# Batched matmul with a transposed right side: six of GpSimd's fourteen stores moved behind the loads on the SP queue

## The chip, the cores and the metric

The kernel runs on one core of a Trainium2 chip; the program uses no other core. The metric is the device time of one execution in microseconds. The profile's span is about 1.8 us shorter than that time (124.1 against 125.88 us in the profiled execution of the kernel before). Every time quoted here comes from an execution whose trace was recorded.

## The reference

```python
batch, m, k, n = 16, 512, 512, 512          # a: [16, 512, 512], b: [16, 512, 512], f32
def reference(a, b):
    return np.matmul(a, b.transpose(0, 2, 1)).astype(np.float32)
```

The inputs are 33.55 MB and the output 16.78 MB, so 50.33 MB must move whatever is done.

## The kernel before

It works in eight pairs of batches. SP's queue loads 2 MB of `a` or `b` for a pair into one of seven slots `ld`. VectorE casts to bf16, TensorE transposes, VectorE and ScalarE copy the transposes to SBUF, TensorE multiplies, and ScalarE copies the sums from PSUM to one of seven output slots `ob`, 1 MB for each batch. The stores are the part that the change touches. GpSimd runs through the string `STORES`. An S waits until a batch is complete and issues its store. An O waits until the next store in turn has landed and hands its slot back to ScalarE.

```python
    STORES = "SSSSOSOSOSSOSOSOSOSOSOS"        # 14 S, 9 O
    LAST = 2                                  # the last two stores go on SP's queue
    ...
        # SP: loads; "s_go" hands a landed load to VectorE
        for n in range(NL):
            load(n)
        for n in range(2 * pairs):
            got = nc.sync.wait_ge(s_ld[n % NL], 16 * (n // NL + 1))
            ...                               # got.then_inc(s_go, ...)
            if n > 0 and n + NL - 1 < 2 * pairs:
                load(n + NL - 1)
        for n in range(batch - LAST, batch):
            nc.sync.wait_ge(s_out, n + 1)
            nc.sync.dma_start(
                out[n].rearrange("(p j) n -> p j n", j=J), ob[:, n % NO]
            ).then_inc(s_last[n % LAST], 16)
    ...
        # GpSimd: nothing before load 7 has landed, then the string
        nc.gpsimd.wait_ge(s_ld[0], 32)
        for what in STORES:
            if what == "S":
                slot = n_st % NO
                nc.gpsimd.wait_ge(s_out, n_st + 1)
                nc.gpsimd.dma_start(
                    out[n_st].rearrange("(p j) n -> p j n", j=J), ob[:, slot]
                ).then_inc(s_st[slot], 16)
                n_st += 1
            else:
                nc.gpsimd.wait_ge(s_st[n_of % NO], 16 * (n_of // NO + 1)).then_inc(s_of, 1)
                n_of += 1
    ...
    # after the closing barrier: the wait for the last store
        nc.sync.wait_ge(s_last[(batch - 1) % LAST], 16)
```

Of the kernel before, what the change touches and what calls it, by code (L numbers as in the profile page):

```python
# [10 lines left out]
def kernel(  # L11
# [6 lines left out]
    nc = tc.nc  # L18
    P = 128
    batch, M, K = a.shape  # L20
    _, N, _ = b.shape
    J = M // P
# [7 lines left out]
    NO = 7  # L30


    STORES = "SSSSOSOSOSSOSOSOSOSOSOS"
    LAST = 2

    def sbuf(name, shape, dtype):
        return ctx.enter_context(nc.sbuf_tensor(name, shape, dtype))

    def sem(name):
        return tc.alloc_semaphore(name)  # L40

    with tc.tile_critical(no_gpsimd_drain=True):  # L42
# [8 lines left out]
        ob = sbuf("ob", [P, NO, J, N], f32)  # L51
# [3 lines left out]
        s_set = sem("s_set")  # L55
        s_ld = [sem(f"s_ld{i}") for i in range(NL)]
        s_second = [sem(f"s_second{i}") for i in range(2)]
        s_last = [sem(f"s_last{i}") for i in range(LAST)]
        s_st = [sem(f"s_st{i}") for i in range(NO)]

        s_go = sem("s_go")
        s_of = sem("s_of")
# [12 lines left out]
        s_out = sem("s_out")  # L75
# [5 lines left out]
            out=ident[:], in_=ident[:], compare_op=mybir.AluOpType.not_equal, fill=1.0,  # L81
# [7 lines left out]
        def load(n):  # L89
            u, slot = n // 2, n % NL  # L90
            src = (a if n % 2 == 0 else b)[2 * u:2 * u + 2].rearrange(
                "e (p j) k -> (e p) j k", j=2 * J
            )
            if n >= NL:

                nc.sync.wait_ge(s_cd, n - NL + 2)
            if n < 2:
                nc.sync.dma_start(
                    ld[:, slot, :J, :], src[:, :J, :]
                ).then_inc(s_ld[slot], 16)  # L100
                nc.sync.dma_start(
                    ld[:, slot, J:, :], src[:, J:, :]
                ).then_inc(s_second[slot], 16)
            else:
                nc.sync.dma_start(ld[:, slot], src).then_inc(s_ld[slot], 16)

        for n in range(NL):
            load(n)
        for n in range(2 * pairs):
# [6 lines left out]

            if n > 0 and n + NL - 1 < 2 * pairs:
                load(n + NL - 1)

        for n in range(batch - LAST, batch):  # L120
            nc.sync.wait_ge(s_out, n + 1)
            nc.sync.dma_start(
                out[n].rearrange("(p j) n -> p j n", j=J), ob[:, n % NO]
            ).then_inc(s_last[n % LAST], 16)
        for n in range(batch - NO, batch - LAST):
            nc.sync.wait_ge(s_st[n % NO], 16 * (n // NO + 1))
        for n in range(batch - LAST, batch - 1):
            nc.sync.wait_ge(s_last[n % LAST], 16)


        n_st = n_of = 0
        nc.gpsimd.wait_ge(s_ld[0], 32)
        for what in STORES:
            if what == "S":
                slot = n_st % NO
                nc.gpsimd.wait_ge(s_out, n_st + 1)
                nc.gpsimd.dma_start(  # L137
                    out[n_st].rearrange("(p j) n -> p j n", j=J), ob[:, slot]
                ).then_inc(s_st[slot], 16)
                n_st += 1  # L140
            else:
                nc.gpsimd.wait_ge(s_st[n_of % NO], 16 * (n_of // NO + 1)).then_inc(s_of, 1)
                n_of += 1

        def taker(engine):
# [10 lines left out]
        with nc.Fori(0, pairs, engines=[dve]) as u:  # L156
            for x, (h, w, s_c, s_w) in enumerate(
# [4 lines left out]
                if x == 0:  # L162
# [3 lines left out]
                    out=h[:, :J, :], in_=src[:, :J, :HK]  # L166
# [4 lines left out]
                    out=h[:, J:, :], in_=src[:, J:, :HK]  # L171
                ).then_inc(s_c, 1)
                nc.vector.tensor_copy(  # L173
                    out=w[:, J:, :], in_=src[:, J:, HK:]
                ).then_inc(s_w, 1)
            for ko in range(KO):
# [5 lines left out]
                if ko == 1:  # L182
# [3 lines left out]
                    out=tb[:, ko, :],  # L186
# [9 lines left out]
        with nc.Fori(0, pairs, engines=[act]) as u:  # L196
            for ko in range(KO):
# [5 lines left out]
                for e in range(2):  # L203
                    c = nc.scalar.copy(  # L204
                        out=ta[:, ko, e * J * P:(e + 1) * J * P].rearrange(
                            "k (j p h) -> k j p h", j=J, h=2
                        ),
# [5 lines left out]
            for e in range(2):  # L213
                take(s_of, 1)
                dst = ob[:, bass.ds((u * 2 + e) % NO, 1)].rearrange("m o j n -> m (o j) n")
                for j in range(J):
                    if j < J - 1:
                        nc.scalar.wait_ge(s_mm, j + 1)
                    else:
# [3 lines left out]
                        out=dst[:, j, :].rearrange("m (p j) -> m p j", j=2 * J),  # L223
# [51 lines left out]


    with tc.tile_critical(no_gpsimd_drain=True):
        nc.sync.wait_ge(s_last[(batch - 1) % LAST], 16)


# [28 lines left out]
```

## Time and profile before

| | before |
|---|---|
| time, median of 3 | 125.86 us (125.82 to 125.87) |
| span of the profile | 124.1 us |
| data moved, mean rate | 50.33 MB, 406 GB/s |
| last data packet ends, fifteen DMA engines | 120.3 to 120.6 us |
| last data packet ends, the sixteenth | 122.24 us |

The page and the stretches by stage are shown with the prediction, below. Two more views are needed: the DMA issues with the median time from issue to landing, and the waits of SP's queue from 66 us on (who waited, for whom, us in total, times, longest).

```profile
out_dram<-ob POOLq DMA_DIRECT2D x14, 1024.0 KB, 24.1
out_dram<-ob SPq DMA_DIRECT2D x2, 1024.0 KB, 8.3
```

```profile
SPq L110 <- DMA ld<-in_b_dram: 22.2, 3, 7.4
SPq L122 <- ACT ob L222: 13.6, 2, 11.8
SPq L304 <- DMA out_dram<-ob: 1.7, 1, 1.7
```

The reader sees that GpSimd's stores take 24 us each from issue to landing (up to four are issued at once, and they share the engines with the loads), and that the last thing SP waits for, 1.7 us long, is the landing of the last store.

One reading of the trace is used all through this text and needs a name. In these traces a DMA reports its landing by 16 increments of a semaphore (544 for the 34 DMAs of the kernel before), and I read them as one from each DMA engine: of the last store of the kernel before, fifteen come from 120.6 to 121.0 us and one at 122.71, as fifteen engines end by 120.6 and one at 122.24. **The lag** is the time from the last but one of these to the last, read to about 0.01 us. **The excess** of a packet is what it took over the usual time of its size, 309 ns for 8 KB and 611 ns for 16 KB (the medians of the kernel before). The packet records do not number the engines, so the excess is summed over all of them; from 102 us on, the packets with an excess follow one another almost without overlap (from 102 to 114 us of the kernel before, 20 packets have an excess over 10 ns, and no two overlap by more than 13 ns), as those of a single engine do.

### The profile page before, as it was taken

What the parts mean: (1) busy time and instruction counts of PE and PEld (TensorE: products, weight loads), DVE (VectorE), ACT (ScalarE), POOL (GpSimd) and SP (SyncE); (2) the same over time, 40 slices, a digit from 0 to 9 for tenths busy, and PEclk for the clock granted to TensorE, in tenths of its full rate; (3) what the DMA queues carried; (4) which work ended last, traced back from release to release, by engine and by line L of the source; (5) the groups of instructions that cost most, each with busy time, mean ns of one, the idle gap of its engine ahead of it and who ended that gap; (6) DMA issues with size and microseconds to landing.
All of it is one profiled execution on the core that took longest, in us unless ns stands there. A gap on an engine that the chain in (4) does not pass through costs nothing. (4 is left out here: it accounts for less than half of the span.)

```text
span 124.1 us, 2416 instructions
## 1 busy us (share of the span) xinstructions
PE 92.3 (74%) x768; PEld 57.8 (47%) x768; DVE 70.2 (57%) x112; ACT 68.1 (55%) x130; POOL 9.5 (8%) x20
## 2 busy tenths in 40 slices
PE   0006299998999999899989998994699937995000
PEld 0005296467446744764574476343684426541000
DVE  0065677948992896589389478903878059400000
ACT  4005133589568845966695589336665196556000
POOL 2000000000000170002010220101010012100000
PEclk9999999999999999999999999999679999999965
DMA  4999999999999999999999999999999999999980
GB/s 79 401 428 431 452 423 438 423 428 423 433 433 423 428 433 396 433 407 449 417 428 449 409 441 425 420 441 420 449 415 417 428 431 428 425 425 423 428 338 11
DMA packets 4896, 50.33 MB, mean 406 GB/s; under 512 B 544, under 2 KB 544, under 8 KB 544
## 3 DMA queue, kind: packets, MB, share of 16 engines
q1 hardware_dynamic: 2880, 35.65, 68.2%
q0 software_dynamic: 2016, 14.68, 28.1%
HBM read 33.55 MB, written 16.78 MB: 406 GB/s over the span
## 5 line engine op out<-in xcount | busy, mean ns | idle before, releaser
L264 PE MATMUL ps<-tb,ta 128*128 128x512 bf16 x256 | 57.7, 379 | 0.4
L222 ACT COPY ob<-ps 128x512 f32 x64 | 34.4, 589 | 29.4 <-PE ps L264 26.2
L204 ACT COPY ta<-tp 128x512 bf16<-128x512 bf16 x64 | 32.9, 608 | 15.7 <-PE tp L245 15.7
L264 PEld LDWEIGHTS ps<-tb,ta 128*128 128x128 bf16 x256 | 24.1, 98 | 30.5 <-issue 3.9
L245 PE MATMUL tp<-ident,ha 128*128 128x128 bf16 x256 | 20.2, 236 | 12.5 <-PEq L146 12.5
L245 PE MATMUL tp<-ident,hb 128*128 128x128 bf16 x256 | 19.3, 235 | 8.3 <-PEq L146 8.2
L245 PEld LDWEIGHTS tp<-ident,ha 128*128 128x128 bf16 x256 | 17.5, 107 | 15.7 <-issue 14.0
L185 DVE COPY tb<-tp 128x1024 bf16<-128x1024 bf16 x32 | 21.3, 685 | 5.0 <-DVEq L146 4.8
L245 PEld LDWEIGHTS tp<-ident,hb 128*128 128x128 bf16 x256 | 17.1, 107 | 9.0 <-issue 9.0
L137 POOL DMA_DIRECT2D out_dram<-ob x14 | 8.8, 631 | 95.7 <-DMA out_dram<-ob 54.3
L165 DVE CAST hb<-ld 128x1024 bf16 x8 | 5.5, 688 | 12.8 <-DVEq L146 12.8
L180 DVE COPY ha<-wa 128x2048 bf16<-128x2048 bf16 x8 | 5.6, 694 | 10.1 <-DVEq L146 9.8
L165 DVE CAST ha<-ld 128x1024 bf16 x8 | 5.5, 690 | 6.6 <-DVEq L146 6.4
L170 DVE CAST hb<-ld 128x1024 bf16 x8 | 5.5, 685 | 1.1 <-DVEq L146 1.1
L170 DVE CAST ha<-ld 128x1024 bf16 x8 | 5.5, 688 | 1.0 <-DVEq L146 1.0
L184 DVE COPY hb<-wb 128x2048 bf16<-128x2048 bf16 x8 | 5.5, 685 | 0.5 <-DVEq L146 0.5
L168 DVE CAST wa<-ld 128x1024 bf16 x8 | 5.5, 687 | 0.0
L168 DVE CAST wb<-ld 128x1024 bf16 x8 | 5.5, 685 | 0.0
L173 DVE CAST wa<-ld 128x1024 bf16 x8 | 5.5, 683 | 0.0
L173 DVE CAST wb<-ld 128x1024 bf16 x8 | 5.5, 682 | 0.0
L195 ACT ACT_TABLE_LOAD x1 | 1.3, 1283 | 1.1 <-SPq L42 1.1
L80 POOL TENSOR_SCALAR_AFFINE_SELECT ident<-ident 128x128 bf16<-128x128 bf16 x1 | 0.3, 284 | 0.2 <-POOL ident L78 0.2
(6 smaller groups left out, 0.8 us busy)
## 6 DMA issues: line engine op xcount, KB each, us to landing
ld<-in_a_dram SPq DMA_DIRECT2D x7, 2048.0 KB, 30.1
ld<-in_b_dram SPq DMA_DIRECT2D x7, 2048.0 KB, 31.2
out_dram<-ob POOLq DMA_DIRECT2D x14, 1024.0 KB, 24.1
ld<-in_a_dram SPq DMA_DIRECT2D x2, 1024.0 KB, 6.0
ld<-in_b_dram SPq DMA_DIRECT2D x2, 1024.0 KB, 10.1
out_dram<-ob SPq DMA_DIRECT2D x2, 1024.0 KB, 8.3
```

The source lines that it names most:

```text
L137: nc.gpsimd.dma_start(out[n_st].rearrange("(p j) n -> p j n", j=J), ob[:, slot]).then_inc(s_st[slot], 16)
L165: nc.vector.tensor_copy(out=h[:, :J, :], in_=src[:, :J, :HK]).then_inc(s_cd, 1)
L168: nc.vector.tensor_copy(out=w[:, :J, :], in_=src[:, :J, HK:])
L170: nc.vector.tensor_copy(out=h[:, J:, :], in_=src[:, J:, :HK]).then_inc(s_c, 1)
L173: nc.vector.tensor_copy(out=w[:, J:, :], in_=src[:, J:, HK:]).then_inc(s_w, 1)
L180: nc.vector.tensor_copy(out=ha[:], in_=wa[:]).then_inc(s_ca, 1)
L184: nc.vector.tensor_copy(out=hb[:], in_=wb[:]).then_inc(s_cb, 1)
L185: nc.vector.tensor_copy(out=tb[:, ko, :], in_=tp[:, 2 + ko % 2].rearrange("k j p -> k (j p)"),).then_inc(s_eb, 1)
L204: c = nc.scalar.copy(out=ta[:, ko, e * J * P:(e + 1) * J * P].rearrange("k (j p h) -> k j p h", j=J, h=2), in_=tp[:, ko % 2, :, e * HP:(e ...
L222: c = nc.scalar.copy(out=dst[:, j, :].rearrange("m (p j) -> m p j", j=2 * J), in_=ps[:, j, :].rearrange("m (j p) -> m p j", j=2 * J),)
L245: t = nc.tensor.transpose(tp[:, 2 * x + g, j, :], h[:, j, g * P:(g + 1) * P], ident[:])
L264: t = nc.tensor.matmul(ps[:, j, :], ta[:, ko, (e * J + j) * P:(e * J + j + 1) * P], tb[:, ko, :].rearrange("k (j p) -> k j p", j=2 * J)[:, ...
```

## The change

Its intent is to use GpSimd's queue (`software_dynamic` on the page; SP's is `hardware_dynamic`) for the first eight stores only, and to let SP issue the other eight behind the loads. Stores 8 to 13 are placed in SP's loop after the hand-over of loads 11, 13 and 15. Each store gets a semaphore of its own.

```diff
-    STORES = "SSSSOSOSOSSOSOSOSOSOSOS"
-    LAST = 2
+    STORES = "SSSSOSOSOSSOOOOOO"
+    LATE = {11: (8, 9), 13: (10, 11), 15: (12, 13)}
...
+        def store(n):
+            engine = nc.gpsimd if n < STORES.count("S") else nc.sync
+            engine.wait_ge(s_out, n + 1)
+            engine.dma_start(
+                out[n].rearrange("(p j) n -> p j n", j=J), ob[:, n % NO]
+            ).then_inc(s_st[n], 16)
...
             if n > 0 and n + NL - 1 < 2 * pairs:
                 load(n + NL - 1)
-        for n in range(batch - LAST, batch):
-            ...
+            for m in LATE.get(n, ()):
+                store(m)
+        store(batch - 2)
+        store(batch - 1)
...
-                nc.gpsimd.wait_ge(s_st[n_of % NO], 16 * (n_of // NO + 1)).then_inc(s_of, 1)
+                nc.gpsimd.wait_ge(*landed(n_of)).then_inc(s_of, 1)
```

More of the change, by code (lines that the diff above doesn't have):

```diff
@@ L57 @@
         s_second = [sem(f"s_second{i}") for i in range(2)]
-        s_last = [sem(f"s_last{i}") for i in range(LAST)]
-        s_st = [sem(f"s_st{i}") for i in range(NO)]
+        s_st = [sem(f"s_st{i}") for i in range(batch)]
         s_go = sem("s_go")
@@ L105, in load, with landed @@
                 nc.sync.dma_start(ld[:, slot], src).then_inc(s_ld[slot], 16)
+        def landed(n):
+            return s_st[n], 16
+        def store(n):
[4 more added lines that the diff above has]
+            ).then_inc(s_st[n], 16)
         for n in range(NL):
@@ L118 @@
                 load(n + NL - 1)
-        for n in range(batch - LAST, batch):
-            nc.sync.wait_ge(s_out, n + 1)
-            nc.sync.dma_start(
-                out[n].rearrange("(p j) n -> p j n", j=J), ob[:, n % NO]
-            ).then_inc(s_last[n % LAST], 16)
-        for n in range(batch - NO, batch - LAST):
-            nc.sync.wait_ge(s_st[n % NO], 16 * (n // NO + 1))
-        for n in range(batch - LAST, batch - 1):
-            nc.sync.wait_ge(s_last[n % LAST], 16)
+            for m in LATE.get(n, ()):
+                store(m)
+        store(batch - 2)
+        store(batch - 1)
+        for n in range(batch - NO, batch - 1):
+            nc.sync.wait_ge(*landed(n))
         n_st = n_of = 0
@@ L134 @@
             if what == "S":
-                slot = n_st % NO
-                nc.gpsimd.wait_ge(s_out, n_st + 1)
-                nc.gpsimd.dma_start(
-                    out[n_st].rearrange("(p j) n -> p j n", j=J), ob[:, slot]
-                ).then_inc(s_st[slot], 16)
+                store(n_st)
                 n_st += 1
             else:
-                nc.gpsimd.wait_ge(s_st[n_of % NO], 16 * (n_of // NO + 1)).then_inc(s_of, 1)
+                nc.gpsimd.wait_ge(*landed(n_of)).then_inc(s_of, 1)
                 n_of += 1
@@ L277 @@
     with tc.tile_critical(no_gpsimd_drain=True):
-        nc.sync.wait_ge(s_last[(batch - 1) % LAST], 16)
+        nc.sync.wait_ge(*landed(batch - 1))
 _INS = ['a', 'b']
```

## The prediction

> **What bounds the kernel now.** I read the page first, then the stretches by stage, then the waits of the SP queue, then the order of time, and last the trace's records of DMA packets and of the 16 increments by which each DMA reports its landing. The page's first two parts and its DMA rows:
>
> ```profile
> span 124.1 us, 2416 instructions
> ...
> PE 92.3 (74%) x768; PEld 57.8 (47%) x768; DVE 70.2 (57%) x112; ACT 68.1 (55%) x130; POOL 9.5 (8%) x20
> ...
> DMA  4999999999999999999999999999999999999980
> ...
> q1 hardware_dynamic: 2880, 35.65, 68.2%
> q0 software_dynamic: 2016, 14.68, 28.1%
> HBM read 33.55 MB, written 16.78 MB: 406 GB/s over the span
> ```
>
> The reader is to see that no compute engine is near full, while the DMA row is at 9 (90% or more) from the second slice to the last but one. The two queues together hold 68.2 + 28.1 = 96.3% of the time of 16 DMA engines. The kernel is bound by its 50.33 MB, and the change moves not one byte less. The stretches (columns: stretch, its length, busy time and count by engine, granted clock, DMA share, GB/s):
>
> ```profile
> 4.00:43.00 39.00, 29.15 (x259) 20.21 (x260) 25.92 (x41) 20.69 (x40) 0.00 (x0) 1.00 1.01 431
> 47.00:99.00 52.00, 47.68 (x397) 29.30 (x395) 34.01 (x55) 33.39 (x65) 4.35 (x7) 0.97 1.00 427
> 103.00:112.00 9.00, 8.50 (x73) 4.93 (x71) 3.83 (x7) 5.28 (x12) 1.41 (x2) 1.00 1.01 425
> 116.00:118.00 2.00, 0.00 (x0) 0.00 (x0) 0.00 (x0) 0.00 (x0) 0.00 (x0) 1.00 1.03 434
> 118.00:120.20 2.20, 0.00 (x0) 0.00 (x0) 0.00 (x0) 0.00 (x0) 0.00 (x0) 0.62 1.02 432
> 120.70:122.20 1.50, 0.00 (x0) 0.00 (x0) 0.00 (x0) 0.00 (x0) 0.00 (x0) 0.50 0.05 22
> 122.30:124.10 1.80, 0.00 (x0) 0.00 (x0) 0.00 (x0) 0.00 (x0) 0.00 (x0) 0.50 0.00 0
> ```
>
> Loads alone (4 to 43), loads and GpSimd's stores together (47 to 99), GpSimd's stores alone (103 to 112) and the last SP stores (116 to 120.2) all run at 425 to 434 GB/s. So which queue carries a transfer does not set the rate. The sixth row is the one that matters: from 120.7 to 122.2 the DMA share is 0.05, about one sixteenth. **One DMA engine of sixteen works on after the other fifteen are done.** In the packet records the fifteen end between 120.3 and 120.6 us, and one ends at 122.24, finishing packets of 309 ns one by one.
>
> **Where that laggard comes from.** Each DMA reports its landing by 16 increments, one for each engine. For each landing I took the distance of the last increment from the last but one. For loads up to 42.8 us, when no store had yet been issued, it is 0.06 us or less. Then it grows: 0.30 us for the load that lands at 62.9, 0.68 at 77.9, 0.98 at 92.8, 1.09 at 100.2; for GpSimd's stores 1.11 at 102.5, 1.47 at 107.7, 1.69 at 115.3. The two last stores, which SP issues, have 1.69 (120.2) and 1.74 (122.7). So the lag begins when GpSimd's stores begin and is 1.7 us by the end: 1.7 / 14 stores = 0.12 us per store on GpSimd's queue, and between the two SP stores it grows by 0.05 only. The packets themselves do not last longer on GpSimd's queue: its 8 KB packets take 309 ns at the median, and so do the 8 KB packets on SP's.
>
> [...] 427 GB/s with both queues against 431 with one. [...] loads go in 16 KB packets (612 ns), stores in 8 KB packets (309 ns), so a store should get a third of the rate, 1.05 MB / (428 / 3 GB/s) = 7.35 us; GpSimd's stores land at 55.3, 62.6, 69.9, 77.2, 84.6, 91.9, 99.2 us, every 7.3 us. [...] an engine falls behind with GpSimd's stores, but one only, and the records do not number it.
>
> **The change, part by part.**
> 1. Removed from GpSimd's queue: stores 8 to 13, six of fourteen DMAs (631 ns of issue each, 3.8 us on an engine that is 8% busy: worth nothing). Added to SP's queue: the same six, at about 0.35 us of issue each (the two that SP issues now take 343 and 347 ns). No byte, matmul or copy changes; the order of instructions on PE, DVE and ACT is the same.
> 2. The stages until about 99 us: unchanged. GpSimd's queue holds stores 0 to 7, of which store 6 lands at 99.2, so through the whole load phase a store is there to share with the loads, as now. Loads 12 to 15 are in SP's queue since 58.2 us, ahead of the new stores, which are issued after load 11 has landed (70.4). So the last load still lands near 100.2.
> 3. The new waits on SP. SP also hands VectorE its loads, so a wait for a result before the next hand-over could hold the pipeline. After the hand-over of load 11 it waits for batches 8 and 9, whose last copies run 72.5 to 73.6; the next load lands at 77.9: 4.3 us to spare. After load 13 (85.3) it waits for batches 10 and 11, whose copies end at 86.9; the next load lands at 92.8: 5.9 to spare. After load 15 nothing is left to hand over. Cost 0.
> 4. The tail. At about 99 us GpSimd's queue has store 7 and SP's has 8 to 11. Both are 8 KB packets, so they share evenly: a store alone takes 1.05 MB / 428 GB/s = 2.45 us, two together 4.9, so 7 and 8 land at about 104 to 105.3 us, in place of 102.5 and 105.1. ScalarE needs the slot of store 7 at 108.05 (its first copy of batch 14) and that of store 8 near 111.5: no stall. Stores 7 to 11 keep the DMA busy until 99 + 5 x 2.45 = 111.3; 12 and 13 are issued near 102 and cover until 116; 14 and 15 come at 112.1 and 114.3 as now. No gap, so the fifteen engines still end near 120.5.
> 5. The lag of the sixteenth: eight stores on GpSimd's queue instead of fourteen. In proportion 1.7 x 8/14 = 0.97 us. As a cross-check, store 7 of the kernel before landed with 1.11. I take 1.05, so the last engine ends 0.65 us sooner.
> Sum: 125.86 - 0 - 0.65 = 125.2 us (0.5%).
>
> **Rivals.** (a) The lag belongs to stores of any queue, or to the time that loads and stores are mixed[...]. For it: the lag grows most in the mixed phase, and its growth fades at the end. Against it: from 102.5 to 112.8, with no loads left, it still grows from 1.11 to 1.65. It would give 125.8 to 125.9. (b) A new stall: SP held in a wait delays a hand-over, or batch 14 waits for its slot. Against it: the 4.3, 5.9 and some 3 us to spare. If the slot came late by more than that, each us would shift the last two stores and empty the queue: 126.5 to 127.5. (c) Stores on one queue alone run slower than shared ones. For it: only two stores run on SP now. Against it: 434 and 432 GB/s in the rows above, where only they remain at the end. A loss of 2% over the 17 us tail would cost 0.3 us: about 125.5 net. (d) The lag vanishes[...]: at most 1.7 us, 124.2.
>
> **Range and chances.** The centre is 125.2. Rival (a) or (c) sets the upper edge, 125.9; a lag cut by more than in proportion, by about 1.1 us, sets the lower, 124.75. A gain of 2% would need 2.5 us, more than the whole lag, and the rest is bytes at the rate of all stages: chance 0.01. A loss of 2% needs rival (b) at its worst: 0.02.
>
> **What would show it.** Right: the DMA row stays at 9 until the last slices; the SP queue's waits for the copies of batches 8 to 11 end before the next load lands; the last load lands near 100.2; fifteen engines end near 120.5 and the last near 121.6; the distance of the last increment stops growing after GpSimd's last store (about 105 us) at about 1 us. Wrong: that distance goes on growing with SP's stores (rival a), a wait of ScalarE near 108 or a DMA slice below 9 in the tail (b), or a lower rate after 105 us (c).

## The result and the profile after

The changed kernel takes 125.88 us (125.76 to 125.98, 4 runs) against 125.87 us (125.82 to 126.16, 4 runs) for the kernel before. The ratio is 0.9996, with a 95% interval of 0.9977 to 1.0015. A ratio here is the mean time of one kernel's fast runs over that of the other's fast runs of the same rounds, so it is not quite the ratio of the medians. The result is correct.

The page of the changed kernel, the lines that answer to those of the prediction:

```profile
span 124.2 us, 2416 instructions
...
PE 92.5 (74%) x768; PEld 58.0 (47%) x768; DVE 70.0 (56%) x112; ACT 68.1 (55%) x130; POOL 6.2 (5%) x14
...
DMA  4999999999999999999999999999999999999970
...
q1 hardware_dynamic: 3744, 41.94, 80.2%
q0 software_dynamic: 1152, 8.39, 16.0%
HBM read 33.55 MB, written 16.78 MB: 405 GB/s over the span
```

The stretches of the changed kernel, in the same columns as before (stretch, length, busy time and count of PE, PEld, DVE, ACT and POOL, granted clock, DMA share, GB/s):

```profile
4.00:43.00 39.00, 29.05 (x258) 20.23 (x259) 25.68 (x41) 20.45 (x40) 0.00 (x0) 1.00 1.01 430
47.00:99.00 52.00, 47.90 (x398) 29.41 (x396) 34.04 (x55) 33.62 (x65) 2.86 (x4) 0.97 1.01 426
103.00:112.00 9.00, 8.49 (x73) 4.94 (x71) 3.85 (x7) 5.27 (x11) 0.00 (x0) 1.00 1.01 426
116.00:118.00 2.00, 0.00 (x0) 0.00 (x0) 0.00 (x0) 0.00 (x0) 0.00 (x0) 1.00 1.02 430
118.00:120.20 2.20, 0.00 (x0) 0.00 (x0) 0.00 (x0) 0.00 (x0) 0.00 (x0) 0.71 1.01 428
120.70:122.20 1.50, 0.00 (x0) 0.00 (x0) 0.00 (x0) 0.00 (x0) 0.00 (x0) 0.50 0.07 27
122.30:124.10 1.80, 0.00 (x0) 0.00 (x0) 0.00 (x0) 0.00 (x0) 0.00 (x0) 0.50 0.00 0
```

The bytes moved from one queue to the other (GpSimd's share falls from 28.1% to 16.0% of the engines' time), every stage runs at the same rate, and the sixth row is still there. From 120.7 to 122.2 us one DMA engine works alone, as before. Its last packet ends at 122.27 us, before at 122.24.

The waits of SP's queue from 66 us on, and the DMA issues:

```profile
SPq L120 <- DMA ld<-in_b_dram: 22.3, 3, 7.5
SPq L113 <- ACT ob L224: 17.4, 7, 10.1
...
SPq L306 <- DMA out_dram<-ob: 1.7, 1, 1.7
```

```profile
out_dram<-ob POOLq DMA_DIRECT2D x8, 1024.0 KB, 28.7
out_dram<-ob SPq DMA_DIRECT2D x8, 1024.0 KB, 20.4
```

SP now waits seven times for copies of ScalarE, and the closing wait for the last store is again 1.7 us. What the prediction had counted on, a smaller lag, did not come. These are the lags of landings near the same time in the two kernels, in us (up to 100.2 us they are those of loads):

```
landing near      42.8   62.9   77.9   92.8  100.2  105.1  107.8  110.3  112.8  115.3  120.2  122.7
before            0.06   0.30   0.68   0.98   1.09   1.29   1.47   1.57   1.65   1.69   1.69   1.74
after             0.14   0.18   0.61   0.84   1.03   1.30   1.51   1.60   1.64   1.71   1.72   1.76
```

From 105 us on the stores that land are GpSimd's in the kernel before (until 119.6) and SP's in the changed one. The lag grows in the same way. The packet records of the lagging engine show it packet by packet. Each row is one 8 KB packet, a selection of ten: its start, its queue (q0 is GpSimd's, q1 is SP's), how much it took over the usual 309 ns, and how many instructions of all engines began while it ran:

```
before                              after
102.90  q0  +38 ns  18 instr.       102.90  q0  +30 ns  17 instr.
103.57  q0  +52      4              103.59  q0  +52      4
104.91  q0  +38      7              104.94  q1  +47      8
105.58  q0  +43     17              105.61  q1  +43     16
105.92  q0  +52     13              105.96  q1  +52     13
110.09  q0  +26      5              110.11  q1  +26      5
113.58  q0  +24      4              113.60  q1  +24      4
113.91  q0   +0      0              113.93  q1   +0      0
114.52  q0   +0      0              114.55  q1   +0      0
116.36  q1   +0      0              116.39  q1   +0      0
```

The excess stands at the same times whichever queue carries the packet (row by row it does not go with the count of instructions; over whole microseconds it does, as is shown after experiment 8), and it stops at 113.9 us, when ScalarE's last copy runs and the compute engines fall silent. This suggested another cause: **the lagging engine loses time to the instructions that the other engines execute.** The prediction's cause is called theory G below (stores on GpSimd's queue make one DMA engine lag), the new one theory I (instructions make it lag).

### The profile page after: what moved, and what is told of

Read it like the earlier page. It is cut to its first block, busy times and chain, and to the rows that moved or that the text cites. A ratio compares the mean times of both kernels' runs of the same rounds, so it can differ in the third digit from the quotient of the medians.

```text
span 124.2 us, 2416 instructions
## 1 busy us (share of the span) xinstructions
PE 92.5 (74%) x768; PEld 58.0 (47%) x768; DVE 70.0 (56%) x112; ACT 68.1 (55%) x130; POOL 6.2 (5%) x14
## 5 line engine op out<-in xcount | busy, mean ns | idle before, releaser
L247 PEld LDWEIGHTS tp<-ident,ha 128*128 128x128 bf16 x256 | 17.5, 107 | 15.8 <-issue 14.1
L113 POOL DMA_DIRECT2D out_dram<-ob x8 | 5.5, 693 | 65.0 <-DMA ld<-in_b_dram 41.5
```

The lines of the kernel that those rows point to most:

```text
L113: engine.dma_start(out[n].rearrange("(p j) n -> p j n", j=J), ob[:, n % NO]).then_inc(s_st[n], 16)
L247: t = nc.tensor.transpose(tp[:, 2 * x + g, j, :], h[:, j, g * P:(g + 1) * P], ident[:])
```

## The experiments

The kernels of transfers alone give a wrong result; they keep the loads and stores and drop the work. Their output buffer is filled once, by a memset on VectorE that ends at 16 us.

**1. The transfers alone.** The loads, fourteen GpSimd stores and two SP stores of the kernel before, with pacing by landings, and no work.

```diff
-        dve = nc.vector.engine ... act = nc.scalar.engine ... pe = nc.tensor.engine ...   (all loops)
+        nc.vector.memset(ob[:], 1.0).then_inc(s_out, 16)
...
-                nc.sync.wait_ge(s_cd, n - NL + 2)
+                nc.sync.wait_ge(s_ld[slot], 16 * (n // NL))
```

> The kernel before with its loads and its 14 GpSimd and 2 SP stores, but no work on TensorE, VectorE (but for one early memset of the buffer that is stored) or ScalarE; its result is wrong on purpose. Theory G[...]: the last increment of the last landing still trails the last but one by about 1.7 us, time 125.8. Theory I (the instructions that the compute engines execute while stores are in flight make it lag): it trails by under 0.2 us, all sixteen engines end near 120.6, time about 124.2.

The lag of the last landing is 0.02 us, and all sixteen engines end between 120.3 and 120.8 us. All fourteen GpSimd stores were there. The engines start within 0.7 to 1.0 us of one another, so a lag could hide in that order; the durations of the packets can't. Here is the excess of the packets of all engines together, in us:

```
packets that start at      70 to 100 us    100 to 114 us    114 to 120.3 us
before (14 on GpSimd)          0.60            0.70              0.01
after (8 on GpSimd)            0.58            0.73              0.01
transfers alone (14)           0.00            0.00              0.00
```

So theory G falls: GpSimd's stores make no engine lag. The time was expected at 124.2 us and came out at 125.48 us (ratio 0.9977, interval 0.9962 to 0.9992). The reason is at the end of the trace. In this kernel the last DMA to land is GpSimd's store 13, at 121.17 us. SP waits for that one ahead of the closing barrier, so the barrier starts only after it; in the kernel before it starts at 120.5 us, ahead of the last landing. The next run mends this.

**2. The transfers alone, with the same ending.** SP's last two stores are held back, so that they land last.

```diff
+        nc.sync.wait_ge(s_st[11 % NO], 16 * (11 // NO + 1))
         for n in range(batch - LAST, batch):
```

> The transfers alone as in the first such run, but the last two SP stores are held back until GpSimd's store 11 has landed, so that they land last and the closing barrier overlaps them as in the kernel before; wrong result on purpose. Theory I (instructions): no lagging engine, all data done near 120.8 us, span near 122.7, time 124.3 to 124.6 (1.0 to 1.2% faster). If the end of the span does not follow the lag: 125.4 as in the first run.

The time is 124.32 us (124.14 to 124.46, 4 runs), ratio 0.9877 with an interval of 0.9860 to 0.9893. The lag of the last landing is 0.18 us, no more than at 43 us (0.22). The last data end at 120.91 us, 1.33 us sooner than in the kernel before. The stretches of this run (VectorE and GpSimd are its only busy engines, so two pairs of columns):

```profile
118.00:120.20 2.20, 0.00 (x0) 0.00 (x0) 1.00 1.01 428
120.70:122.20 1.50, 0.00 (x0) 0.00 (x0) 1.00 0.00 0
```

The row in which one engine worked alone is empty. Without the work, the whole lag is gone, and with it 1.5 us, about what a cure of the lag could bring. The chip is not the reason: this run and a repeat of the changed kernel (`after_nop200`, experiment 4) were made on the same chip, and the repeat has a lag of 1.39 us.

**3. The transfers and one kind of instruction.** Each of these adds instructions from 43 us on, when the first stores are in flight.

```diff
 # dma_pe1000
+        with nc.Fori(0, 10, engines=[nc.tensor.engine]):
+            for i in range(100):
+                nc.tensor.transpose(tp[:, i % 4, 0, :], ident[:], ident[:])
 # dma_dve1000: unrolled
+        for i in range(1000):
+            nc.vector.memset(scr[:, i:i + 1], 1.0)
```

> The transfers alone, plus 1000 transposes with their weight loads on TensorE from about 43 us on, without semaphores between them; wrong result on purpose. Theory G: same lag as the transfers alone. Theory I: the lag grows while TensorE is busy and stops when it stops, to something between 0.5 and 2.5 us. If only semaphore updates matter and not instructions, it stays under 0.2 us.

> The transfers alone, plus 1000 one-column memsets on VectorE from about 43 us on; wrong result on purpose. Theory G: same lag as the transfers alone. Theory I: the lag grows while VectorE runs, by 1 to 3 ns for each instruction, 1 to 3 us in all. If TensorE alone matters: no growth.

With the transposes two engines end late, 0.90 and 1.19 us after the others. One of them is explained by a single packet of 16 KB at 53.0 us, in a queue of its own, which took 1068 ns; it comes 10 us into the new loop, and the trace names it a fetch of instructions. The other falls behind step by step, 0.17 us at the landing at 62.8, 0.61 at 100, 0.89 at 102.4, and then stays at 0.90 to the end. TensorE stopped at 100.9 us.

With the unrolled memsets the lag is 5.3 us. But here the trace names eight packets as instruction fetches, 8 KB each, one every 5.4 us. Each took a DMA engine 0.31 to 0.33 us, and the store packet that began as it ended took 0.64 to 0.79 us in place of 0.31. This run mixes two things, so it was repeated with a loop:

```diff
 # dma_memset1000, on the kernel of experiment 2
+        with nc.Fori(0, 50, engines=[nc.vector.engine]):
+            for i in range(20):
+                c = nc.vector.memset(scr[:, i:i + 1], 1.0)
+            c.then_inc(s_x, 1)
+            nc.vector.wait_ge(s_x, 1).then_inc(s_x, -1)
```

> The transfers alone (last two stores held back), plus 1000 one-column memsets on VectorE from about 43 us in a loop, so that no instructions need to be fetched by DMA; wrong result on purpose. Theory I (executed instructions slow one DMA engine while stores are in flight): one engine lags by 1 to 3 us, growing while VectorE runs, and flat after it. If the lag of 5.4 us in the unrolled run was all fetching: under 0.3 us.

In this loop the trace names no packet a fetch of instructions. The lag grows from 0.10 us at 42.8 us to 0.67 at 99.8 and is 0.69 at the end. VectorE stopped at 94.8 us. It is less than the 1 to 3 us that I expected, and well above the 0.3 us of the other case. So 4.6 of the 5.3 us of the unrolled run went with being unrolled, that is, as I read it, with the fetching of its instructions, and 0.6 us (0.69 - 0.10) is the price of executing 1000 of them, mostly while loads and stores share the engines.

**4. Does the instruction have to touch memory?** A loop of no-operations was to tell, but the build left the no-operations out, and only the loop's 50 rounds of branch and register instructions ran, until 55.8 us.

```diff
 # dma_nop1000 (and after_nop200, the same on the changed kernel)
+            for i in range(20):
+                nc.vector.nop()
```

> The same, plus a loop of 1000 no-operations on VectorE from about 43 us: no data, no semaphores, no new instructions to fetch. If an engine's access to SBUF or the fetch of instructions is what slows the one DMA engine: no lag. If executing any instruction is: a lag of 0.5 to 3 us.

> The changed kernel, with a loop of 200 no-operations on VectorE after its last copy (107.4 us), its result right. Theory I with any instruction counting: the lag goes from 1.7 to 2.0 or more and the time up by as much. With only data-moving instructions counting: no change.

The lags of the last landing were 0.03 us and, on the changed kernel, 1.39 us; neither run tests what it was made for. The second serves as a repeat of the changed kernel: its excess is 0.58 us from 70 to 100 and 0.73 from 100 to 114, as in the first profile, though its lag is 0.37 us smaller. I take it that the lag of one profile depends also on where in the order the slow engine started, which no run was made to show; the excess is the steadier measure. The replacement uses semaphores, which the build kept:

```diff
 # dma_sem1000
+        with nc.Fori(0, 50, engines=[nc.vector.engine]):
+            for i in range(10):
+                nc.vector.nop().then_inc(s_ea, 1)
+                nc.vector.wait_ge(s_ea, 1).then_inc(s_ea, -1)
```

> The transfers alone, plus a loop on VectorE with 500 semaphore increments and 500 semaphore waits from about 43 us, which read and write no memory; wrong result on purpose. If every executed and recorded instruction costs: a lag of 1 us or more. If only instructions that touch SBUF or PSUM cost: under 0.3 us.

The 1000 semaphore instructions ran from 43 to 158 us, so the span of 159.9 us tells nothing, but the landings do. The lag is 0.13 us at 42.9, 0.34 at 99.6, 0.40 at 101.8 and 1.09 at 122.1. In the last 20 us, with stores alone in flight, the engine lost 0.69 us to 175 of these instructions and 18 of the loop itself, 3.5 to 4 ns each. In the program these instructions have no tile in SBUF or PSUM to read or write. So an instruction needs no data there to be in the way.

**5. Does it need stores in flight?** 600 transposes were put into the stage of loads alone.

```diff
 # dma_pe_early
+        nc.tensor.wait_ge(s_ld[0], 16)
+        with nc.Fori(0, 6, engines=[nc.tensor.engine]):
+            ...                               # 100 transposes
```

> The same, with 600 transposes on TensorE from about 6 us, while only loads are in flight, and none later. If the slowing needs stores in flight: no lag at the end (under 0.3 us). If it does not: about 0.6 us of lag already at 43 us, as 0.6 of the lag of the run with 1000 transposes.

Neither expectation was met as written. One 16 KB packet at 15.8 us, again named a fetch of instructions, in a queue of its own and 1034 ns long, made one engine 1.26 us late at the landing at 19.6 us. After that the lag did not grow: 1.29 us at 44.1. The transposes, on from 6.2 us to 41.9, are one group in order of time:

```profile
6.18 35.68 PE L149 MATMUL tp<-ident 128*128 128x128 bf16 x600 [6.18 <-DMA ld<-in_a_dram]
```

So while some 370 transposes ran between 19.6 and 41.9 us (at 59 ns each) and only loads moved, this lag grew by 0.03 us, where 1000 cost an engine 0.9 us when stores were in flight. The engine that made the fetch need not be the one that instructions slow (in `dma_pe1000` they are two), but no other engine fell behind either, or the lag would have shrunk. The kernel before shows the same: TensorE is busy for 8 or 9 tenths of every slice from 20 to 43 us, and the lag at 42.8 us is 0.06. The slowing needs stores in flight.

**6. The real kernel with more instructions.** 300 memsets (in a first attempt) and then 140 follow VectorE's last copy, when only SP's stores are left.

```diff
 # after_tail140; after_tail300 has 15 rounds
+        with nc.Fori(0, 7, engines=[nc.vector.engine]):
+            ...                               # 20 memsets and a semaphore, as above
```

> The changed kernel, result right, with 300 one-column memsets in a loop on VectorE after its last copy (about 107.5 us), when only SP's stores are left. Theory I: the lag passes 1.7 us and ends near 2.2 to 2.6, time up by 0.5 to 0.9 us. Theory G[...]: unchanged.

> The changed kernel, result right, with 140 one-column memsets in a loop on VectorE after its last copy, which end near 116.5 us, well before the last landing (the loop of 300 ran on beyond it, so its time told nothing). Theory I: last increment behind the undisturbed engines by 2.0 to 2.3 us in place of 1.76, time up by 0.2 to 0.6 us, 126.1 to 126.5. Theory G: 1.76 and 125.9.

The 300 ran on to 126 us, past the last landing, and the closing barrier waited for them: 129.67 us, ratio 1.0292 (1.0251 to 1.0332), which says nothing of the DMA. The lag did come out as expected, 2.30 us from the undisturbed engines. The 140 ended in time:

```profile
120.70:122.20 1.50, 0.00 (x0) 0.00 (x0) 0.00 (x0) 0.00 (x0) 0.00 (x0) 0.50 0.07 27
122.30:124.10 1.80, 0.00 (x0) 0.00 (x0) 0.00 (x0) 0.00 (x0) 0.00 (x0) 0.50 0.01 5
```

The second row of this kernel is no longer empty: the engine works on until 122.65 us. The last increment comes 2.25 us after the undisturbed engines (one other is 0.4 us late, after one 8 KB fetch), in place of 1.76. The time is 126.36 us (126.16 to 126.48), ratio to the kernel before 1.0041 (1.0028 to 1.0054). The lag is 0.49 us larger and the time 0.48 us (126.36 - 125.88). As one repeat had a lag of 1.39, the close match of the two is partly luck; the time, with its interval, and the excess carry this run: from 100 us on the excess is 1.19 us in place of 0.78, without the one packet that the fetch delayed.

**7. The real kernel with all sixteen stores on GpSimd's queue.**

```diff
-    STORES = "SSSSOSOSOSSOSOSOSOSOSOS"
+    STORES = "SSSSOSOSOSSOSOSOSOSOSOSSS"
-        for n in range(batch - LAST, batch):  # SP's two stores
-            ...
```

> The kernel before with all sixteen stores on GpSimd's queue, result right. Theory G: the lag grows with the last two stores as well, to 16 x 0.12 = 1.95 us, 126.1 us. Theory I: 1.7 to 1.8 us as with fourteen and with eight, 125.9.

The last increment comes 1.73 us after the undisturbed engines (two others are 0.2 us late). With sixteen, fourteen and eight GpSimd stores the lag is 1.73, 1.74 and 1.76 us, and the excess of the packets from 100 to 114 us is 0.69, 0.70 and 0.73 us. The time is 126.03 us (125.84 to 126.21), ratio 1.0014 (1.0002 to 1.0026). Taken alone the time lies between the two theories' figures, but its last landing is at 122.70 us, where that of the kernel before is at 122.71. The 0.2 us come after it: in the closing barrier GpSimd's drain lasts until 123.40 us (before: 121.78), and GpSimd's next instruction begins at 123.45 in place of 123.22.

**8. Giving the lagging engine less to do.** The last store was cut, to give the engines unequal shares. Which engine gets which share was my assumption, not shown by a run made before. In both expectations the first figures are for the case that the lagging engine gets a smaller share of the last store, the next for the case that it gets a larger one.

```diff
 # after_split15: the last store
+            for lo, hi in ((0, P),) if n < batch - 1 else ((0, 120), (120, P)):
+                engine.dma_start(dst[lo:hi], ob[lo:hi, n % NO]).then_inc(s_st[n], 16)
 # after_relief7: the last store
+            (0, P, 0, 3), (0, 49, 3, J), (49, 98, 3, J), (98, 123, 3, J), (123, P, 3, J)
```

> The changed kernel, with the last store cut into 120 partitions[...] and 8 partitions[...]. [...] about 1.4 us faster than now, 124.4. [...] 125.9 to 126.3.

> The changed kernel, result right, with the last store cut so that the DMA engines get unequal shares: three quarters of each partition's row in one DMA over all sixteen engines, the last quarter in four DMAs of 49, 49, 25 and 5 partitions[...]. [...] last data near 121.7 us and 0.3 to 0.6 us faster than the changed kernel, 125.3 to 125.6. [...] 126.5 to 127. If small pieces cost more than they save: about 126.

Both are slower. The first takes 126.32 us, ratio 1.0053 (1.0039 to 1.0067). The last engine did not end sooner (from 122.3 to 124.1 us data still moved at 5 GB/s, in the changed kernel at 0), and the 8 KB packets of the last store took up to 647 ns in place of 309. Why is open; the second run did not show it (84 ns for all but 5 of its 128 packets of 2 KB). The second takes 127.51 us, ratio 1.0146 (1.0123 to 1.0170), and shows why. After its last 6 KB packet (until 121.70 us) the lagging engine moved exactly twenty 2 KB packets of 84 ns, the last ending at 123.3 us. An even share would be 128 / 16 = 8, so this cut gave the lagging engine more to do and not less. No version here beats both kernels.

**The count over all traces.** The kept traces allow one more test, without a new run. For three stages, here are the excess of all packets (less the one that a fetch delayed in `after_tail140`), the instructions of the program that began, those of the sequencers included, and the quotient:

```
stores alone, 102 to 114 us           excess us   instructions   ns each
before (14 stores on GpSimd)             0.62          228          2.7
after (8)                                0.65          226          2.9
all_gpsimd (16)                          0.61          228          2.7
after_tail140                            1.00          361          2.8
dma_sem1000                              0.42          122          3.5
dma_only                                 0.00            1           -
loads and stores, 70 to 100 us
before                                   0.60          649          0.9
after                                    0.58          650          0.9
dma_pe1000                               0.89         1096          0.8
dma_memset1000                           0.42          565          0.7
dma_only                                 0.00           16           -
loads alone, 20 to 43 us
before                                   2.04          578           -
dma_pe_early                             1.99          791           -
dma_only                                 2.09            8           -
```

With stores alone the excess goes with the number of instructions, whichever engine executes them and whichever queue the stores use; in slices of 1 us from 102 to 114 us of the kernel before the two correlate with 0.93. Beside loads an instruction costs about a third of that, and with loads alone the excess does not depend on the instructions: its 2 us are there in every kernel, without work too.

## Why the prediction was wrong

The time lies inside the range, but only because rival (a) had set its upper edge; the forecast gain of 0.65 us is not there. By the prediction's steps:

- **What bounds the kernel**: right. It is the bytes, at 426 to 430 GB/s in every stage of the changed kernel, and then one DMA engine alone for 1.7 us.
- **Part 1, issue on GpSimd and SP**: right, no effect. GpSimd's busy time falls from 9.5 to 6.2 us.
- **Part 2, the stages until 99 us**: right. The last load lands at 100.24 us (before 100.22).
- **Part 3, SP's waits**: right. The stores for which SP waited are issued at 71.7, 73.9, 85.7 and 87.1 us; the next loads land at 77.9 and 92.8.
- **Part 4, the tail**: right. Stores 7 and 8 land at 104.8 and 105.1 us, as forecast, and share evenly (91 packets of each queue begin from 99.0 to 102.5 us); ScalarE's first copy of batch 14 begins at 108.08 (before 108.05); fifteen engines end between 120.3 and 120.7.
- **Part 5, "The lag of the sixteenth: eight stores on GpSimd's queue instead of fourteen"**: wrong, and the gain with it. The step "1.7 / 14 stores = 0.12 us per store on GpSimd's queue" took two things that begin together for cause and effect. At 43 us GpSimd's queue starts, and with it stores of any kind start for the first time while the engines compute. The runs showed that the lag comes of the second, stores beside a working core, and not of the queue: no excess at all and 0.02 us of lag with fourteen GpSimd stores and no work, 1.73 to 1.76 us of lag with sixteen, fourteen or eight of them and the work.
- **Rival (a)** was right on the time, 125.8 to 125.9, and half right on the cause (stores of any queue). The argument that I put against it, that the lag "still grows from 1.11 to 1.65" with no loads left, was sound, but it did not speak for GpSimd: until 113.9 us the engines were computing as well. That the growth fades before the last stores was in the trace of the kernel before; I named it and did not ask what else stopped there.
- **Rivals (b) and (c)** did not happen, as argued. **Rival (d)**'s size, 1.7 us with the lag gone, was near: experiment 2 won 1.5 us.

What stays open is how an instruction takes time from a DMA engine. An explanation has to fit what the runs show: it needs no data in SBUF or PSUM (0.69 us lost to the semaphore instructions of `dma_sem1000`), it goes with the number of instructions (2.7 to 3.5 ns each with stores alone), and it needs stores in flight (with loads alone, 2.04 us of excess with 578 instructions and 2.09 with 8), though from 70 to 100 us of the kernel before 0.35 of the 0.60 us of excess is on packets of loads. Every run here was recorded by the profiler. Whether the recording has a part in it, and whether the lag exists when nothing is recorded, no run here shows; a kernel run without the recording would.

## What to carry to other kernels

Before a share of a wait is put down to one queue or engine, list everything that starts and stops at the same times as it does, and look at least at the place where one of them stops alone. In a DMA-bound kernel compare the sixteen engines with one another, not only their sum: one that ends late sets the end (here 1.7 us after the other fifteen), and a stretch with a DMA share of 0.05 to 0.07 was its mark here. Moving plain transfers between queues changed nothing here, where both queues already ran at the rate of the engines (425 to 434 GB/s in the stages shown until 120.2 us). While stores are in flight, count the instructions too: in these recorded runs each cost one DMA engine about 3 ns with stores alone and about 1 ns beside loads.
